# The second weight slab of the next job, split half a product ahead of its old place

## The chip, the cores and the metric

The kernel runs on one core of a Trainium2 chip. The metric is the device time of one execution in microseconds (us); lower is better. A program that is run again gives a slightly different time, so a median of runs is used, and one execution was also taken with the hardware profiler.

The engines are named as the profile names them: PE (the matrix engine), PEld (its weight loads), DVE (the vector engine), ACT (the scalar engine), POOL (GpSimd), SP (the engine whose queue issues most DMAs). Each engine takes its own instructions strictly in the order in which the program issued them to it, and waits only where an input is not there or a buffer is not free.

## The reference, cut to what matters

Two layers of a diffusion-style trunk over 512 latent tokens and, in the first layer, 256 context tokens of width 1024:

```python
for l in range(2):
    h, hc = trunk_layer(h, hc, ...)
def trunk_layer(x, ctx, ...):
    z_lat = split_proj(jnp.dot(layer_norm(x) * (1.0 + sc_l) + sh_l, w_in) + b_in)
    z_ctx = split_proj(jnp.dot(layer_norm(ctx) * (1.0 + sc_c) + sh_c, w_in) + b_in)
    ...
    y_f = fourier_mix(z_lat[0], fnet_w)
    y_d = diff_attn_latent(dq_l, ..., lam, diff_subln, lambda_init)
    y_p = pool_mix(z_lat[6], pool_w, pool_scale)
    y_n = na_latent(...)
    out_lat = gate_and_merge(z_lat, (y_f, y_d, y_p, y_n), w_branch, w_out)
    x_new = layer_norm(alpha * x + g_l * out_lat, ln_g, ln_b)
```

All is float32. Most of the work is products with the weights `w_in` (1024 x 10240), `w_branch` and `w_out`.

## The kernel before, in words

A float32 matrix is taken as the sum of a rounded "high" part and a "low" remainder, and a product as three matmuls: high by high, high by low, low by high. The normalised tokens lie on chip as such a pair (tiles `px0h`, `px0l` or `px1h`, `px1l`). The weights come in slabs of 512 rows by 256 columns (512 KB). A slab is fetched into one of three raw buffers (`w_raw`, DMA at line 319 in SP's queue). ACT then casts each of its two halves to the high part (`w_hi`, line 339), and DVE or POOL subtracts to get the low part (`w_lo`, line 342). There are four buffers for the split pair. Which engine subtracts is fixed per kind of job and half: both halves on POOL for the token sections (`tok`, `tok2`) and the plain sections (`nat`); the first half on POOL and the second on DVE for `rope` and `out`; both on DVE for gate sections, `merge`, `mgate`, `mproj`.

The program is a list of jobs, each a product of all tokens with some slabs:

- `tok2` and `tok`: token tiles of 128 rows are the outer loop; one "unit" is one tile by 256 columns, eight steps `k` of three matmuls
- `nat`, `rope`, `mgate`: two products `f` = 0, 1 of 128 weight columns each, eight steps `k` of three passes over all tokens (768 in layer 0, 512 in layer 1 for most)
- `merge`: two gate products and two branch products, three slabs; `mproj`: one slab
- `out`: units again. In layer 0 the token tiles fall in a first group of four tiles and a second of two; in layer 1 in two groups of two tiles. So a job has four units in the one case, and two in the three others; the last job of layer 1 has two column blocks, four units and four slabs

Most jobs use two slabs, here A (rows 0 to 511, needed from `k` = 0) and B (from `k` = 4). While a job runs, `ws.ahead(1)` splits A of the next job and `ws.ahead(2)` splits B. A split does this at its place in the program: it issues the raw DMA of the slab two further on (in a buffer that the slab just before the split one frees, and whose split is forced to its end first if it is not done), casts the first half on ACT, and starts a small chain: 0.6 planner-us later the subtraction of the first half and the cast of the second, 0.6 later the subtraction of the second. The planner's clock counts matmul time alone, 0.32 per step `k` of a unit.

All other work is placed by the same clock. After each step, chains that are due are issued (`pump`), and side work, that is the Fourier branch, differential attention and neighbourhood attention, is issued piece by piece between the steps of the section jobs. In the `out` jobs, evacuation of a unit is on DVE (multiply from the accumulator, line 1633; add the residual `xs`, line 1636; statistics, line 1639), and when a token tile has all its columns, a row chain `end_row` normalises it: small DVE steps, a power on POOL (line 578), a scaling on ACT (line 1656), a multiplication by `lng` (line 1659, on POOL for the four tiles of the first group), an addition on DVE (line 1662), and in layer 0 a second normalisation, transposes on PE (line 278), a scaling on ACT (line 606) and the split into the next layer's pair on DVE. The residual tiles `xs` have three buffers, and are fetched from SP's queue at the head of each unit.

Of the kernel before, what the change touches and what calls it, by code (L numbers as in the profile page):

```python
# [109 lines left out]
def emit(tc, A, out):  # L110
# [41 lines left out]
    def group(l, g):  # L152
        t = toks(l)
        return t[:-2] if g == 0 else t[-2:]
# [8 lines left out]
    for j in J:  # L163
# [7 lines left out]
        elif j[0] in ("merge", "mgate", "mproj"):  # L171
            _, l, b, s = j
# [9 lines left out]
    with ExitStack() as ctx, tc.manual_schedule():  # L182
# [30 lines left out]
        def finish(c, upto=None):  # L213
            while c.i < (len(c.st) if upto is None else upto):
                one(c)
# [50 lines left out]
        def mmt():  # L266
            return ring("mm", psA, [128, 512])
# [12 lines left out]
        def mm3(o, ah, al, bh, bl, start, stop):  # L280
            mm(o, ah, bh, start, False)
            mm(o, ah, bl, False, False)
            mm(o, al, bh, False, stop)
# [130 lines left out]
        ws = Stream(early)  # L414
# [204 lines left out]
        def gen_T(ps, hs, cols, X, chunks, nk, after=None, before=None):  # L619
            for k in range(nk):  # L620
                if before:
                    before(k)
                wh, wl = hs[k // 4]
                wh, wl = wh[:, k % 4, cols], wl[:, k % 4, cols]
                for j, (o, n) in enumerate(chunks):
                    mm(ps[j][:, :n], wh, X[0][:, k, o:o + n], k == 0, False)
                yield
                for j, (o, n) in enumerate(chunks):
                    mm(ps[j][:, :n], wh, X[1][:, k, o:o + n], False, False)
                yield  # L630
                for j, (o, n) in enumerate(chunks):
                    mm(ps[j][:, :n], wl, X[0][:, k, o:o + n], False, k == nk - 1)
                if after and k == after[0]:
                    after[1]()
                yield

        def chunks(n):
            return [(0, 512), (512, 256)] if n == T0 else [(0, 512)]
# [47 lines left out]
        def bias_row(l, c0):  # L686
            bb = sm.tile([128, 256], F32, name="bb", tag="bb")
            nc.sync.dma_start(bb, A["b_in"][l:l + 1, c0:c0 + 256].broadcast_to([128, 256]))
            return bb

        def job_tok(l, sec, s, X, F):
            hs = ws.take(2)
            bb = bias_row(l, sec * 512 + s * 256)
            tl = [4, 5, 0, 1, 2, 3] if (sec != 0 or l == 0) else [0, 1, 2, 3]
            for t in tl:
                if t == tl[0]:
                    mid = lambda: ws.ahead(1)
                else:
                    mid = (lambda: ws.ahead(2)) if t == tl[-1] else None
                yield from tok_unit(l, sec, s, t, X, F, hs, bb, mid)  # L700

        def job_tok2(l, sec, X, F):

            hs = ws.take(2)
            bb = [bias_row(l, sec * 512 + s * 256) for s in range(2)]
            for t in [4, 5, 0, 1, 2, 3]:
                if l == 0:
                    need(f"xt{t}")
                else:
                    finish_cls("out")  # L710
                    finish(rows_[t])
                finish(xt[t])
                for s in range(2):
                    if t == 4 and s:
                        hs += ws.take(2)
                    yield from tok_unit(l, sec, s, t, X, F, hs[2 * s:2 * s + 2], bb[s],
                                        (lambda: ws.ahead(2)) if (t == 3 and s == 1) else None)

        def evac_rope(l, sec, g, ps, ch, n, b, mt, cos, sin):

# [37 lines left out]
        def job_nat(l, sec, s, X, mt, tables=None):  # L758
            hs = ws.take(2)
            n = T0 if (sec in (3, 9) or l == 0) else NL  # L760
            ch = chunks(n)
            for f in range(2):
                ps = [mmt() for _ in ch]
                yield from gen_T(ps, hs, slice(f * 128, (f + 1) * 128), (X.h, X.l), ch, 8,
                                 after=((3, lambda: ws.ahead(1)) if f == 0 else (5, lambda: ws.ahead(2))))
                ct = sec * 4 + s * 2 + f
                b = biasT[l][:, ct:ct + 1]
                if sec in (2, 3):
                    evac_rope(l, sec, 2 * s + f, ps, ch, n, b, mt, *tables)
                elif sec in (8, 9):  # L770
                    evac_qk(l, sec, s, f, ps, ch, n, b, mt)
                elif sec == 6:
                    pool_group(l, 2 * s + f, ps, ch, n, b, mt)
                else:
                    evac_gate(l, sec, s, f, ps, ch, n, b, mt)
# [212 lines left out]
        def finish_cls(name):  # L988
            for c in klass.get(name, []):
                finish(c)  # L990
# [533 lines left out]
        def gate(l, b, dt_, ps, ch, sg):  # L1524
            ct = 48 + BR[b] * 8 + dt_

            def sig():
                for j, (o, m) in enumerate(ch):
                    S.activation(sg[:, o:o + m], ps[j][:, :m], AF.Sigmoid, bias=biasT[l][:, ct:ct + 1])  # L1529

            return chain((0.4, sig), hold=ps)
# [40 lines left out]
        def job_mgate(l, b, s, X, mp, sgs):  # L1572
            n = TQ[l]
            hs = ws.take(2)
            ch = chunks(n)
            for f in range(2):
                ps = [mmt() for _ in ch]
                yield from gen_T(ps, hs, slice(f * 128, (f + 1) * 128), X, ch, 8,
                                 after=((3, lambda: ws.ahead(1)) if f == 0 else (5, lambda: ws.ahead(2))))
                dt_ = 2 * s + f  # L1580
                sgs[dt_] = mp.tile([128, T0], F32, name="sgs", tag=("sg", "sg", "mtmp", "mtmp", "my", "my", "mg", "mg")[dt_], bufs=2)
                gate(l, b, dt_, ps, ch, sgs[dt_])
# [23 lines left out]
        def job_out(l, g, qs, M, ep, yt, gb, bst, lng, lnb):  # L1606
            hs_ = ws.take(2 * len(qs))
            units = [(t, q) for t in group(l, g) for q in qs]
            rows = list(gate_rows(l, gb, ep)) if (g, qs) == (0, (0,)) else []
            for i, (t, q) in enumerate(units):  # L1610
                cs = slice(q * 256, (q + 1) * 256)
                hs = hs_[2 * (q - qs[0]):][:2]
                ts = slice(t * 128, (t + 1) * 128)
                xs = ep.tile([128, 256], F32, name="xs", tag="xs", bufs=3)
                src = hres[ts, cs] if l else (A["x"][0, ts, cs] if t < 4 else A["ctx"][0, (t - 4) * 128:(t - 3) * 128, cs])
                nc.sync.dma_start(xs, src)
                ps = mmt()
                for k in range(8):
                    wh, wl = hs[k // 4]
                    mm3(ps[:, :256], M.h[:, k, ts], M.l[:, k, ts], wh[:, k % 4, :], wl[:, k % 4, :], k == 0, k == 7)  # L1620
                    if k == 3:
                        if i == 0 and len(qs) == 1:
                            ws.ahead(1)
                        if i == len(units) - 1:
                            ws.ahead(2)
                    if k % 2 == 0 and k // 2 < len(rows) and i < 2:
                        rows[k // 2][i]()
                    yield
                y = yt[t][:, cs]

                def gate_(y=y, ps=ps, t=t, cs=cs):
                    finish_cls("gate")
                    V.tensor_tensor(out=y, in0=ps[:, :256], in1=gb[0 if t < 4 else 1][:, cs], op=ALU.mult)  # L1633

                def add(y=y, xs=xs):
                    V.scalar_tensor_tensor(out=y, in0=xs, scalar=ALPHA, in1=y, op0=ALU.mult, op1=ALU.add)  # L1636

                def stats(y=y, t=t, q=q):
                    V.bn_stats(bst[t][:, q, :], y)
                    if q == 3:  # L1640
                        rows_[t] = end_row(l, t, yt[t], bst[t], lng, lnb, ep)

                chain(((3.6, 1.8)[i] if rows and i < 2 else 0.4, gate_), (0.41, add), (0.4, stats), hold=[ps], cls="out", depth=1)
# [105 lines left out]
        def need(flag):  # L1749
            while flag not in flags:  # L1750
                if not side_step(True):
                    assert pend, (flag, want)
                    finish(pend[0])
                    raise_flags()
# [28 lines left out]
        for j in J:  # L1783
# [81 lines left out]
            elif kind == "rope":  # L1865
                if not cs_:
                    need("fw")
                    late_tables()
                drive(job_nat(l, j[2], j[3], X, mt, cs_))
            elif kind == "nat":  # L1870
                drive(job_nat(l, j[2], j[3], X, mt))
# [65 lines left out]
```

## Time and profile before

| | us |
|---|---|
| runs | 2005.49, 2010.09, 2010.26 |
| their median | 2010.09 |
| the profiled execution, its own time | 2006.96 |
| its span, first to last instruction | 2005.2 |
| mean granted clock of PE, share of full speed | 0.976 |

The profile is one execution. Its page gives each engine's busy time; other views of the same trace list what each engine waited for ("waits"), the busy time in a stretch ("windows"), and the instructions in order of time ("timeline"). An idle stretch carries, after an arrow, the instruction that ended it. In the timeline a row may stand for several equal instructions in succession (x2, x3).

### The profile page before, as it was taken

Reading aid. Unit: us, or ns where it says so; the run is one execution under the profiler, and the core shown is the slowest. Engines: PE = TensorE matmul, PEld = TensorE weight load, DVE = VectorE, ACT = ScalarE, POOL = GpSimd, SP = SyncE. Lnnn points to the kernel's source line nnn. Section 1 sums busy time; section 2 is a strip of 40 time slices with the busy share of each in tenths; the row PEclk is TensorE's granted clock in tenths of the full one; section 3 lists DMA queues with packets and bytes.
Section 4 is the critical chain, followed back from the end, with each engine's and each line's share of the span. In section 5 each row is a group of like instructions: output and inputs, shape, how many; then the busy total and the mean of one; then the engine's idle time right before and its main releaser. Section 6 shows DMA issues by size and latency. Waiting matters only on the chain.

```text
span 2005.2 us, 30691 instructions
## 1 busy us (share of the span) xinstructions
PE 1901.0 (95%) x11703; PEld 1653.8 (82%) x11703; DVE 1185.4 (59%) x2369; ACT 861.7 (43%) x1673; POOL 329.9 (16%) x322
## 2 busy tenths in 40 slices
PE   6999999997999999999999979998999999999996
PEld 4998888776888888888888979877877887888886
DVE  7635676563666444656537784577655664465267
ACT  5423365564666422212223354355555664333232
POOL 6321121101120000000001443122122210000023
PEclk8999999998999999999999979999999999999999
DMA  8433844435453524434322446364327645444344
GB/s 275 132 103 108 250 135 152 161 108 163 154 160 106 181 96 136 137 107 152 99 95 96 132 150 193 103 237 137 124 100 236 210 135 183 136 159 137 94 132 152
DMA packets 257394, 293.71 MB, mean 146 GB/s; under 512 B 25844, under 2 KB 220384, under 8 KB 256736
## 3 DMA queue, kind: packets, MB, share of 16 engines
q1 hardware_dynamic: 256672, 286.46, 44.5%
q0 software_dynamic: 576, 5.29, 0.7%
q8 instruction: 92, 1.51, 0.3%
q14 instruction: 54, 0.44, 0.1%
HBM read 230.82 MB, written 62.35 MB: 146 GB/s over the span
## 4 chain that ended last, share of the span: by engine, by line
PE 52%; DVE 7%; DMA 2%; ACT 2%; issue 2%; POOL 1%; SPq 1%; POOLq 0%; ACTq 0%; DVEq 0%
PE mm L274 46%; PE sd L274 4%; PE sd L278 1%; DVE yt L1636 1%; DVE w_lo L342 1%; DMA w_raw<-in_w_out 1%; PE mm L394 1%; DVE px0l L286 1%; DVE dp L1013 1%; DMA mtmp<-y 1%; ACT px0l L1104 0%; DMA px0h<-nv1h 0%; DVE dp L1030 0%; DVE yt L1633 0%; DMA w_vec<-in_w_mod 0%
## 5 line engine op out<-in xcount | busy, mean ns | idle before, releaser
L342 POOL TENSOR_TENSOR w_lo<-w_raw,w_hi 128x512 fp32r<-128x512 f32 x148 | 209.3, 1425 | 1202.0 <-ACT w_hi L339 1129.6
L339 ACT CAST w_hi<-w_raw 128x512 fp32r<-128x512 f32 x456 | 263.6, 618 | 184.5 <-PE mm L274 120.3
L274 PE MATMUL mm<-px0h,w_hi 128*128 128x512 f32 x1216 | 336.4, 349 | 3.7 <-ACT px0h L1485 3.3
L274 PE MATMUL mm<-px0h,w_lo 128*128 128x512 f32 x1216 | 335.8, 349 | 0.0
L274 PE MATMUL mm<-px0l,w_hi 128*128 128x512 f32 x1216 | 334.1, 347 | 0.4 <-DVE px0l L1489 0.4
L342 DVE TENSOR_TENSOR w_lo<-w_raw,w_hi 128x512 fp32r<-128x512 f32 x308 | 220.1, 735 | 152.0 <-ACT w_hi L339 149.9
L274 PE MATMUL mm<-px1h,w_hi 128*128 128x512 f32 x864 | 291.8, 374 | 1.4 <-ACT sg L1529 1.4
L274 PE MATMUL mm<-px1h,w_lo 128*128 128x512 f32 x864 | 288.0, 369 | 0.0
L274 PE MATMUL mm<-px1l,w_hi 128*128 128x512 f32 x864 | 287.6, 369 | 0.0
L274 PEld LDWEIGHTS mm<-px0h,w_hi 128*128 128x128 f32 x1216 | 192.0, 190 | 34.5 <-ACT px0h L1485 4.5
L274 PEld LDWEIGHTS mm<-px0h,w_lo 128*128 128x128 f32 x1216 | 191.4, 190 | 32.2 <-issue 1.2
L274 PEld LDWEIGHTS mm<-px0l,w_hi 128*128 128x128 f32 x1216 | 192.4, 190 | 30.7 <-DVE px0l L1489 1.5
L274 PEld LDWEIGHTS mm<-px1h,w_hi 128*128 128x128 f32 x864 | 149.5, 189 | 30.6 <-ACT sg L1529 1.9
L274 PEld LDWEIGHTS mm<-px1h,w_lo 128*128 128x128 f32 x864 | 149.5, 189 | 28.3 <-issue 1.3
L274 PEld LDWEIGHTS mm<-px1l,w_hi 128*128 128x128 f32 x864 | 149.6, 189 | 26.8 <-issue 0.5
L274 PE MATMUL mm<-w_hi,px0h 128*128 128x256 f32 x480 | 143.1, 298 | 4.3 <-DVE px0h L610 4.0
L274 PE MATMUL mm<-w_lo,px0h 128*128 128x256 f32 x480 | 139.3, 290 | 6.7 <-POOL w_lo L342 6.0
L274 PE MATMUL mm<-w_hi,px0l 128*128 128x256 f32 x480 | 138.9, 289 | 0.7 <-DVE px0l L286 0.7
L274 PE MATMUL mm<-w_lo,px1h 128*128 128x256 f32 x384 | 112.5, 293 | 8.4 <-DVE w_lo L342 4.7
L274 PE MATMUL mm<-w_hi,px1h 128*128 128x256 f32 x384 | 114.2, 297 | 2.1 <-ACT w_hi L339 1.7
L274 PE MATMUL mm<-w_hi,px1l 128*128 128x256 f32 x384 | 111.5, 290 | 0.2 <-DVE px1l L286 0.2
L1529 ACT ACTIVATE sg<-mm,biasT 128x512 f32<-128x512 f32 x72 | 41.8, 615 | 153.8 <-PE mm L274 123.3
(240 smaller groups left out, 3100.2 us busy)
## 6 DMA issues: line engine op xcount, KB each, us to landing
w_raw<-in_w_in SPq DMA_DIRECT2D x160, 512.0 KB, 4.2
w_vec<-in_w_mod SPq DMA_DIRECT2D x32, 512.0 KB, 3.6
w_raw<-in_w_branch SPq DMA_DIRECT2D x32, 512.0 KB, 3.5
w_raw<-in_w_out SPq DMA_DIRECT2D x32, 512.0 KB, 3.5
w<-in_w_mod SPq DMA_DIRECT2D x12, 512.0 KB, 6.2
g<-ab SPq DMA_DIRECT2D x16, 384.0 KB, 2.7
nb<-bt SPq DMA_DIRECT2D x48, 128.0 KB, 4.5
y<-y SPq DMA_DIRECT2D x14, 384.0 KB, 3.7
```

What stands on the lines that cost most here:

```text
L274: PE.matmul(o, a, b, start=start, stop=stop)
L278: PE.transpose(o, i, idn)
L286: V.tensor_tensor(out=out_lo, in0=src, in1=hi.bitcast(F32), op=ALU.subtract)
L339: S.copy(x[1], x[0])
L342: e.tensor_tensor(out=x[2], in0=x[0], in1=x[1].bitcast(F32), op=ALU.subtract)
L394: PE.matmul(st["p"][:, 4 * b + 2 * v:4 * b + 2 * v + 2], acc[:, v, b * 128:(b + 1) * 128], ones[:, 0:2].bitcast(F32), start=True, stop=True)
L1013: V.tensor_scalar(out=p, in0=src, scalar1=-0.125, scalar2=None, op0=ALU.mult, op1=ALU.min, accum_out=mn)
L1529: S.activation(sg[:, o:o + m], ps[j][:, :m], AF.Sigmoid, bias=biasT[l][:, ct:ct + 1])
L1636: V.scalar_tensor_tensor(out=y, in0=xs, scalar=ALPHA, in1=y, op0=ALU.mult, op1=ALU.add)
```

## The change

`ws.ahead(2)`, the split of slab B of the next job, is issued earlier in five places. Everything else, and the place of `ws.ahead(1)`, stays:

```diff
 (job_tok)
-                    mid = (lambda: ws.ahead(2)) if t == tl[-1] else None
+                    mid = (lambda: ws.ahead(2)) if t == tl[-3] else None
 (job_tok2)
-                                        (lambda: ws.ahead(2)) if (t == 3 and s == 1) else None)
+                                        (lambda: ws.ahead(2)) if (t == 2 and s == 1) else None)
 (job_nat, and the same line in job_mgate)
-                                 after=((3, lambda: ws.ahead(1)) if f == 0 else (5, lambda: ws.ahead(2))))
+                                 after=((3, lambda: ws.ahead(1)) if f == 0 else (1, lambda: ws.ahead(2))))
 (job_out)
-                        if i == len(units) - 1:
+                        if i == max(len(units) - 3, 0):
                             ws.ahead(2)
```

In a `tok` job the place is two units earlier, in `tok2` one tile (two units), in `nat`, `rope` and `mgate` four steps `k` earlier within the second product. In an `out` job of four units it is two units earlier; in one of two units it goes from the second unit to the first, right behind `ws.ahead(1)` of the same step. The split of B forces the chain of A to its end there, since B's raw DMA wants A's buffer. `merge` and `mproj` jobs are not touched.

## Rows read from the trace of the kernel before

**Rows 1.** The page of the profile: busy time, share of the span and instructions of each engine.

```profile
PE 1901.0 (95%) x11703; PEld 1653.8 (82%) x11703; DVE 1185.4 (59%) x2369; ACT 861.7 (43%) x1673; POOL 329.9 (16%) x322
```

**Rows 2.** The waits of PE over the whole run: who waited for what, us in total, times, longest.

```profile
PE mm L274 <- POOL w_lo L342: 15.1, 9, 3.7
PE sd L274 <- DVE px0l L286: 12.2, 11, 3.5
PE sd L274 <- DVE px1l L286: 9.5, 10, 3.0
PE sd L278 <- DVE np L1329: 8.5, 4, 4.0
PE mm L274 <- DVE w_lo L342: 6.6, 6, 3.2
PE mm L274 <- ACT w_hi L339: 5.2, 4, 2.6
```

**Rows 3.** The same view by stretches, columns as before: first three rows from 0 to 52 us, the next three from 1139 to 1183, one from 1183 to 1226, the last two from 1935 to the end.

```profile
PE mm L274 <- POOL w_lo L342: 5.6, 4, 2.4
PE mm L274 <- ACT w_hi L339: 3.5, 3, 2.6
PE mm L274 <- DVE w_lo L342: 1.2, 2, 0.6
...
PE mm L274 <- POOL w_lo L342: 6.0, 2, 3.7
PE sd L278 <- ACT yt L1656: 3.7, 1, 3.7
PE mm L274 <- DVE w_lo L342: 0.7, 1, 0.7
...
PE mm L274 <- POOL w_lo L342: 2.8, 2, 1.8
...
PE mm L274 <- DVE w_lo L342: 4.7, 3, 3.2
PE mm L274 <- ACT w_hi L339: 1.7, 1, 1.7
```

**Rows 4.** Windows: start and end, length, busy us (and instructions) of PE, PEld, DVE, ACT, POOL, then the granted PE clock, the DMA engines' share and GB/s.

```profile
1144.60:1189.60 45.00, 31.86 (x202) 30.43 (x201) 39.86 (x75) 27.72 (x56) 26.54 (x19) 0.79 0.41 130
...
1968.10:1989.70 21.60, 14.46 (x99) 13.43 (x98) 15.65 (x29) 5.78 (x10) 10.07 (x7) 0.92 0.47 152
```

**Rows 5.** The timeline of ACT: start us, us, engine, line, operation, tiles, shapes, count, and the idle time before it. The first row is the last step of `tok2` in layer 0, the others the four-unit `out` jobs of layer 0.

```profile
89.32 1.14 ACT L339 CAST w_hi<-w_raw 128x512 fp32r<-128x512 f32 x2 [0.58 <-PE mm L274]
...
1114.59 1.14 ACT L339 CAST w_hi<-w_raw 128x512 fp32r<-128x512 f32 x2 [8.94 <-PE mm L274]
...
1126.11 1.14 ACT L339 CAST w_hi<-w_raw 128x512 fp32r<-128x512 f32 x2 [8.94 <-PE mm L274]
```

**Rows 6.** The timeline of POOL in the two-unit `out` jobs of layer 0, and one row of PE's. Same columns.

```profile
1141.72 1.47 POOL L342 TENSOR_TENSOR w_lo<-w_raw,w_hi 128x512 fp32r<-128x512 f32 x1
...
1144.12 3.00 POOL L1659 TENSOR_TENSOR yt<-yt,lng 128x1024 f32<-128x1024 f32 x1
1147.08 1.44 POOL L342 TENSOR_TENSOR w_lo<-w_raw,w_hi 128x512 fp32r<-128x512 f32 x1
...
1148.58 0.39 PE L274 MATMUL mm<-w_lo,px0h 128*128 128x256 f32 x1 [2.27 <-POOL w_lo L342]
...
1150.58 3.01 POOL L1659 TENSOR_TENSOR yt<-yt,lng 128x1024 f32<-128x1024 f32 x1
1153.56 1.48 POOL L342 TENSOR_TENSOR w_lo<-w_raw,w_hi 128x512 fp32r<-128x512 f32 x1
```

**Rows 7.** The timeline of the last `out` jobs of layer 1, rows of ACT, DVE and SP (whose rows are the issue of a DMA). Same columns.

```profile
1965.16 1.13 ACT L339 CAST w_hi<-w_raw 128x512 fp32r<-128x512 f32 x2
...
1971.40 1.64 ACT L339 CAST w_hi<-w_raw 128x512 fp32r<-128x512 f32 x3
...
1974.20 1.41 DVE L342 TENSOR_TENSOR w_lo<-w_raw,w_hi 128x512 fp32r<-128x512 f32 x1
...
1976.58 1.05 DVE L1636 SCALAR_TENSOR_TENSOR yt<-xs,yt 128x256 f32<-128x256 f32 x1
1977.67 0.43 DVE L1639 BATCH_NORM_STATS2 st<-yt 128x6 f32<-128x256 f32 x1
1978.01 0.67 DVE L342 TENSOR_TENSOR w_lo<-w_raw,w_hi 128x512 fp32r<-128x512 f32 x1
...
1978.75 0.38 SPq L319 DMA_DIRECT2D w_raw<-in_w_out  x1
...
1984.96 1.66 ACT L339 CAST w_hi<-w_raw 128x512 fp32r<-128x512 f32 x3 [3.70 <-DMA w_raw<-in_w_out]
```

**Rows 8.** The timeline of DVE in the four-unit `out` jobs of layer 0 (first and second row) and at the head of the two-unit ones (third). Same columns.

```profile
1102.05 0.42 DVE L1636 SCALAR_TENSOR_TENSOR yt<-xs,yt 128x256 f32<-128x256 f32 x1
...
1105.73 1.33 DVE L342 TENSOR_TENSOR w_lo<-w_raw,w_hi 128x512 fp32r<-128x512 f32 x1
...
1139.49 2.55 DVE L1636 SCALAR_TENSOR_TENSOR yt<-xs,yt 128x256 f32<-128x256 f32 x1
```

**Rows 9.** The timeline of ACT in a section job of layer 0 with differential attention beside it: the copy of a transposed tile, and behind it the casts of a slab B. Same columns.

```profile
431.97 0.80 ACT L1104 CAST px1l<-sd 128x768 fp32r<-128x768 f32 x1 [0.71 <-PE sd L278]
432.67 1.14 ACT L339 CAST w_hi<-w_raw 128x512 fp32r<-128x512 f32 x2
```

More of the change, by code (lines that the diff above doesn't have):

```diff
@@ L1578, in job_mgate @@
                 yield from gen_T(ps, hs, slice(f * 128, (f + 1) * 128), X, ch, 8,
-                                 after=((3, lambda: ws.ahead(1)) if f == 0 else (5, lambda: ws.ahead(2))))
+                                 after=((3, lambda: ws.ahead(1)) if f == 0 else (1, lambda: ws.ahead(2))))
                 dt_ = 2 * s + f
```

## The prediction, made before the changed kernel was run

> **What bounds the kernel now.** I read the page first: PE is busy 1901.0 of 2005.2 us, so all its idle time together is 104 us [rows 1]. A change that issues the same work in another order can only take from that, or from stretches where PE ran at its lower clock. Next I read what PE waited for. Weights are the smaller part: 15.1 us for low parts from POOL, 6.6 from DVE and 5.2 for high parts from ACT, 26.9 together. Inputs of the side work's products make 12.2, 9.5 and 8.5 [rows 2]. Then the same view by stretches, to see where the weight waits lie: 5.6 + 3.5 + 1.2 = 10.3 us in the first 52 us, where `mod` jobs run that the change leaves alone; 6.7 from 1139 to 1183 and 2.8 from 1183 to 1226; and from 1935 on 4.7, 1.7 and what is left, 26.9 - 10.3 - 6.7 - 2.8 - 6.4 = 0.7 [rows 3]. So from 52 to 1139 and from 1226 to 1935, where most of the moved splits are, PE never waits for a weight: slab B is in time there already. The change can gain directly only at the two `out` phases and at the head of layer 1.
>
> Those places are not PE's alone. From 1144.6 to 1189.6 DVE is busy 39.86 of 45.0 us and PE 31.86, at a mean granted clock of 0.79. From 1968.1 to 1989.7 DVE has 15.65 and PE 14.46 of 21.6 [rows 4].
>
> **The change part by part.** No instruction is added or removed; each moved split takes along one raw DMA in SP's queue, two casts on ACT and two subtractions.
>
> *Four-unit `out` jobs, `tok2`.* Nothing. ACT runs ahead of PE here, and its casts begin when PE has read the old slab in the buffer for the last time: 8.94 us idle until PE, at 1114.59 and again 11.52 us later [rows 5]. That is one job of four units, so a unit takes 2.88 us, and a half slab, two of its eight steps, 0.72. An earlier place in the program changes no such release. In `tok2` the cast at 89.32 already waits for PE's last use [rows 5]; after the change the same wait stands ahead of two evacuation casts in ACT's order, and DVE and SP wait behind these for some 6 us. Four accumulators, 4 x 2.88 = 11.5 us of units, hide that; without them it would cost up to 2.9, one unit, in each layer.
>
> *Two-unit `out` jobs of layer 0.* POOL's order is: first half of A (1141.72), a row's multiplication (1144.12, 3.00 us), first half of B (1147.08). PE stands 2.27 us for the last, then 0.7 for DVE's half [rows 3, 6]. Planner times put B's half behind A's and ahead of that multiplication after the change: ready at 1141.72 + 1.47 + 1.44 = 1144.6, wanted at 1148.58 - 2.27 = 1146.3. Both waits go, 2.97 us. The following job's longest wait, 6.0 - 2.27 = 3.7, is for its B behind a second multiplication [rows 3], and goes in the same way. What is late next is that job's A: it stays behind the multiplication of 1150.58 and is ready at 1153.56 + 1.48 = 1155.0 [rows 6], and PE, without waits, would want it after two units from 1144.6, at 1150.4. So up to 4.6 of 6.7 us comes back. The wait of 3.7 for `yt` (transposes behind the row chain) I take to shorten by 1, bounds 0 and 3.7; of the 2.8 at the head of layer 1, where `tok2`'s B comes late, I take 1.5, bounds 0 and 2.8 [rows 3]. Sum: 6.7 - 4.6 + 1 + 1.5 = 4.6. Its upper bound is 45.0 - 39.86 = 5.1 while DVE's busy time stays [rows 4]; its lower one 6.7 - 4.6 = 2.1, or nothing if A's wait also slows the clock. I take 4.5.
>
> *Last `out` jobs of layer 1.* B's first half is cast with A's second (1965.16, x2), its second only at 1971.40, behind a row's scaling, and DVE subtracts that at 1974.20 to 1975.6; PE waits 4.7 in all for DVE [rows 3, 7]. Moved up, its cast comes behind A's, and its subtraction goes in DVE's order ahead of an addition, an evacuation and a row's two long steps, which I put at 1970.1. It is wanted 6 steps of 0.36 after 1968.1, at 1970.3: about 4 us of waiting go. But the last slab's DMA is issued (1978.75) when DVE has subtracted from the slab whose buffer it takes (1978.01), lands 6.2 us later, and PE waits for that too [rows 3, 7]. DVE has no idle time up to there, so the release moves only past one residual addition and one statistics step, 1.05 + 0.43 = 1.5 us earlier. Less crowded, its DMA could land sooner: up to 4 in all. I take 2.5 between 1.5 and 4.
>
> *Sections and `mgate`.* Forecast: nothing. Cover is PE's own matmuls: a B split late costs no wait today, and one split earlier has more slack. On ACT the pair of casts (1.14 us) moves from one place among the attention's copies to another [rows 9]. In tok 10, nat 9 and 8, and the gate sections, 14 jobs a layer, 28 pairs run beside attention. A pair may leave the path of a copy that PE waits for or step into one: bounds ±28 x 1.14 = ±32 us; the direct waits that it can lengthen or shorten are 30.2 [rows 2]. With no reason for a sign I take 0, ±3.
>
> *SP's queue.* In a two-unit job, the second unit's `xs` now comes behind B's DMA, which waits for A's last subtraction. DVE is late itself there, so I put nothing; without that cover at most 1 us in each of 10 jobs (four in layer 0, six in layer 1).
>
> Sum: 4.5 + 2.5 = 7.0. From the profiled execution's 2006.96 that gives 2000.0. The median shown is 3.1 above that execution; I set the forecast halfway, **2001.5 us**, with a range of its own of 1996 to 2005.
>
> **The rivals.** *One: DVE stays the bound.* DVE's work isn't less, and now A's DVE half runs while POOL works on B's first half. A subtraction took 1.33 us in such company and 0.67 without [rows 7, 8], so six two-unit jobs (four of layer 0, the last two of layer 1) give back 6 x 0.66 = 4.0 of the 7.0: 2004 on the execution's scale, 2005.5 on mine. For it: the residual addition of 0.42 took 2.55 while POOL multiplied, and DVE is full there [rows 4, 8]. Against it: half of these meetings exist today. The Trainium skill says the same, as a rule, in "SBUF — State Buffer", section "Who interferes with whom": a DVE instruction with two SBUF inputs and a GpSimd one that reads SBUF shut each other out whole. By that rule back-to-back halves cost as much as this rival says, and the 2.55 us agrees with it.
>
> *Two: slower.* B's casts land ahead of attention copies on ACT, for which PE then stands. It has to happen, net, to more than 7.0 / 1.14 = 6 of the 28 pairs to eat the gain; with 13 it costs 14.8 - 7.0 = 7.8, 2015 on the execution's scale, 2016 on mine. For it: PE already waits 30.2 us for such inputs, so that chain has no slack [rows 2]. Against it: pairs stand among those copies today as well, such as the one right behind a copy at 432.67 [rows 9], and moving them frees as many places as it fills.
>
> *Three: all goes.* The waits of 6.7, 3.7, 2.8 and 7.1 vanish, 20.3 us, nothing coming back: 1988. Against it: the late A worked out above, and the last DMA.
>
> *That the move does nothing* in the places that count, since engines run at the release of buffers, is the four-unit case; with two units the order on POOL and DVE decides, so I leave it within the first rival.
>
> **How the numbers follow.** Forecast 0.45, rival one 0.27 (2004 to 2010, taking in no effect), two 0.20 (2010 to 2024), three 0.08 (1985 to 1995). A measurement of this kernel tells about 0.3%, 6 us, from no change, so faster means below 2004.1 and slower above 2016.1. Faster: 0.8 of the forecast's chance, all of three, little of one: 0.36 + 0.08 + 0.01 = 0.45. Slower: 0.8 of rival two and a little of mishap beside: 0.17. Same: 0.38. The range 1992 to 2012 leaves out about 0.05 below and 0.13 above.
>
> **What would show it.** In the changed kernel's profile the POOL wait of 2.27 at the first unit of layer 0's second two-unit job must be gone, with the multiplication now behind two subtractions; a wait for A of the next job should appear near 1151. In layer 1 the wait near 1975 for DVE's low part should shrink to under 1 us, and the last slab's DMA be issued 1 to 2 us sooner relative to the end. If PE's weight waits after 1139 still add up to over 12 us, rival one holds or the order isn't what I worked out; if waits for px or np parts exceed 38 us in all, rival two.

## The result, and the profile of the changed kernel

| | us |
|---|---|
| the changed kernel, median of 6 runs | 2025.80 (2019.60 to 2029.74) |
| the kernel before, median of 6 runs | 2009.71 (2005.49 to 2011.26) |
| ratio of the two | 1.0078, 95% interval 1.0061 to 1.0096 |
| profiled execution, its own time; span; mean granted clock | 2021.72; 2019.9; 0.978 |

The change made the kernel slower by 0.78 per cent, some 16 us. The forecast was 2001.5 us, a gain, with a range that ended at 2012.

Busy time by engine of the changed kernel, the first part of its page, answering to [rows 1]:

```profile
PE 1902.0 (94%) x11703; PEld 1656.2 (82%) x11703; DVE 1190.6 (59%) x2369; ACT 860.4 (43%) x1673; POOL 330.4 (16%) x322
```

PE's own work is the same within 1 us, and DVE takes 5.2 us longer over its instructions. What grew is waiting. The waits of PE over the whole run (who for whom, us in total, times, longest), answering to [rows 2]:

```profile
PE mm L274 <- POOL w_lo L342: 15.4, 9, 4.5
PE sd L274 <- DVE px1l L286: 11.5, 9, 3.0
PE sd L274 <- DVE px0l L286: 11.5, 11, 3.1
PE sd L278 <- DVE np L1329: 7.2, 4, 3.8
PE sd L278 <- ACT yt L1656: 7.0, 3, 3.7
PE mm L274 <- ACT w_hi L339: 7.0, 4, 3.3
PE mm L274 <- DVE vt L654: 5.6, 2, 3.4
...
PE mm L274 <- DVE w_lo L342: 4.6, 5, 1.5
```

Three things are to be seen. The inputs of attention, 11.5 + 11.5 + 7.2 = 30.2 us, are what they were. Waits for weights, 15.4 + 7.0 + 4.6 = 27.0, are too (26.9 before): the change removed some and made others. New are `vt`, 5.6 us, which is PE waiting for an accumulator that DVE has not evacuated, and `yt`, the scaled row that PE transposes, 7.0 instead of 3.7.

Where the time went, worked out from the end of the last matmul of each stage in the two traces:

| stage | difference, us |
|---|---|
| `mod` | -2.4 |
| `tok2` and the first `tok` jobs, layer 0 | +4.4 |
| rest of layer 0 up to the `out` jobs | +0.9 |
| `out` of layer 0, `tok2` of layer 1 | +5.9 |
| first `tok` jobs, layer 1 | +5.1 |
| rest of layer 1 up to the `out` jobs | -1.1 |
| `out` of layer 1 | +1.9 |

They add up to the 14.7 by which the spans differ. The first line is no effect of the change: the traces of all kernels below show it too, -0.9 to -2.5. One trace against one other is not exact in the long section stages: in kernels whose edit leaves the sections alone a layer's sections differ from the kernel before by -1.8 to +7.2.

**The head of each layer.** The chain is told by a few rows of three timelines (start us, us, engine, line, operation, tiles, count, idle time before; SPq and the DMA rows are the issue of a transfer). First the changed kernel:

```profile
82.03 8.99 SPq L319 DMA_DIRECT2D w_raw<-in_w_in  x2
87.38 1.14 ACT L339 CAST w_hi<-w_raw 128x512 fp32r<-128x512 f32 x2 [6.34 <-PE mm L274]
...
93.36 0.52 SPq L832 DMA_DIRECT2D pw<-in_pool_w  x1
93.43 0.75 POOL L898 DMA_DIRECT2D px1h<-in_k_tabh  x1
93.97 0.56 SPq L688 DMA_DIRECT2D bb<-in_b_in  x1
94.18 0.53 POOL L899 DMA_DIRECT2D px1l<-in_k_tabl  x1
...
104.82 0.42 DVE L654 TENSOR_TENSOR vt<-mm,bb 128x256 f32<-128x256 f32 x1 [7.18 <-DMA bb<-in_b_in]
105.30 0.39 PE L274 MATMUL mm<-w_hi,px0h 128*128 128x256 f32 x1 [2.18 <-DVE vt L654]
...
1249.18 0.36 PE L274 MATMUL mm<-w_hi,px1h 128*128 128x256 f32 x1 [3.39 <-DVE vt L654]
```

Then the kernel before, whose PE was some 2 us later at this point:

```profile
90.10 2.86 SPq L319 DMA_DIRECT2D w_raw<-in_w_in  x2
93.05 0.46 SPq L832 DMA_DIRECT2D pw<-in_pool_w  x1
93.60 0.45 SPq L688 DMA_DIRECT2D bb<-in_b_in  x1
...
95.19 0.75 POOL L898 DMA_DIRECT2D px1h<-in_k_tabh  x1
95.94 0.54 POOL L899 DMA_DIRECT2D px1l<-in_k_tabl  x1
...
98.82 0.42 DVE L654 TENSOR_TENSOR vt<-mm,bb 128x256 f32<-128x256 f32 x1 [3.23 <-DMA bb<-in_b_in]
```

In `tok2` the moved split issues its raw DMA early. The buffer of that DMA comes free only when POOL has subtracted slab A, POOL waits for ACT's casts of A, and these wait until PE has done with the old slab (ACT idle for 6.34 us, until 87.38). So SP, which takes its queue in order, is held for 9 us. Behind it stand four stores, the pool weights `pw`, and `bb`, the bias row of the next job. Before, `bb` (128 KB) was issued 1.6 us ahead of the two Fourier tables (1292 KB each, from POOL's queue), and DVE had it 5.2 us later (98.82 - 93.60). Now it is issued 0.5 us behind the first table, and DVE has it after 10.9 us. DVE cannot evacuate without it; four accumulators last for 11.5 us of units, and PE stands for 2.18 us, then runs 3.4 us at half its clock (granted 0.50, 1.2 of 2.4 GHz). In layer 1 the same chain costs 3.4 us of waiting (the row at 1249.18).

**The two-unit `out` jobs.** PE's waits from 1139 to 1235, answering to rows 4 to 7 of [rows 3]:

```profile
PE mm L274 <- POOL w_lo L342: 8.4, 3, 4.5
PE sd L278 <- ACT yt L1656: 7.0, 3, 3.7
PE mm L274 <- ACT w_hi L339: 1.9, 1, 1.9
```

Before, these were 6.7 + 2.8 for weights and 3.7 for `yt`, 13.2 together; now they are 17.3. The waits of 2.27 and 0.7 for B are gone, and that job ends 4.8 us earlier against its predecessor. The next job gives it all back, and more: PE waits for its A, 1.92 for the high part and 3.37 for the low one. Rows of ACT and PE:

```profile
1155.19 1.24 ACT L1656 ACTIVATE yt<-yt,nm,rs 128x1024 f32<-128x1024 f32 x1 [5.29 <-DVE nm L589]
1156.33 2.16 ACT L339 CAST w_hi<-w_raw 128x512 fp32r<-128x512 f32 x4
1156.99 0.39 PE L274 MATMUL mm<-w_hi,px0h 128*128 128x256 f32 x1 [1.92 <-ACT w_hi L339]
...
1160.74 0.58 PE L274 MATMUL mm<-w_lo,px0h 128*128 128x256 f32 x1 [3.37 <-POOL w_lo L342]
...
1986.87 0.82 ACT L1656 ACTIVATE yt<-yt,nm,rs 128x512 f32<-128x512 f32 x1 [5.76 <-DVE nm L589]
1987.59 2.17 ACT L339 CAST w_hi<-w_raw 128x512 fp32r<-128x512 f32 x4
```

All four casts, A's and B's, stand behind a row scaling for which ACT waited 5.29 us, and that scaling waits for the row's mean from DVE. In layer 1 (the last two rows) it is much the same picture: the job before the last gains 5.0 us and the last one loses 6.0, with four of its casts behind a scaling at 1986.87 that had waited 5.76 us for DVE, and a stretch of 6.83 us at half clock (the granted clock from 1997.41 to 2004.24 is 0.50).

### The profile page after: what moved, and what is told of

Same layout as the page of the kernel before. It is cut to its first block, busy times and chain, and to the rows that moved or that the text cites. A ratio compares the mean times of both kernels' runs of the same rounds, so it can differ in the third digit from the quotient of the medians.

```text
span 2019.9 us, 30717 instructions
## 1 busy us (share of the span) xinstructions
PE 1902.0 (94%) x11703; PEld 1656.2 (82%) x11703; DVE 1190.6 (59%) x2369; ACT 860.4 (43%) x1673; POOL 330.4 (16%) x322
## 3 DMA queue, kind: packets, MB, share of 16 engines
q0 software_dynamic: 576, 5.29, 0.7%
## 5 line engine op out<-in xcount | busy, mean ns | idle before, releaser
L274 PE MATMUL mm<-w_lo,px1h 128*128 128x256 f32 x384 | 113.0, 294 | 10.7 <-POOL w_lo L342 7.2
L274 PEld LDWEIGHTS mm<-w_hi,px0h 128*128 128x128 f32 x480 | 97.2, 202 | 12.8 <-DVE px0h L610 4.5
```

What stands on the lines that cost most here:

```text
L274: PE.matmul(o, a, b, start=start, stop=stop)
```

## The experiments

All ratios are against the kernel before, run beside them; one per cent is 20.1 us.

**Which of the moves costs?** Three kernels, each with a part of the change alone:

```diff
 (tok2_only)
-                                        (lambda: ws.ahead(2)) if (t == 3 and s == 1) else None)
+                                        (lambda: ws.ahead(2)) if (t == 2 and s == 1) else None)
 (out_only)
-                        if i == len(units) - 1:
+                        if i == max(len(units) - 3, 0):
 (sections_only)
-                    mid = (lambda: ws.ahead(2)) if t == tl[-1] else None
+                    mid = (lambda: ws.ahead(2)) if t == tl[-3] else None
-                                 after=((3, lambda: ws.ahead(1)) if f == 0 else (5, lambda: ws.ahead(2))))
+                                 after=((3, lambda: ws.ahead(1)) if f == 0 else (1, lambda: ws.ahead(2))))
```

> Only the place in tok2 is moved. Theory Q (SP's queue): the raw DMA of the moved split holds SP for some 9 us, the bias row bb of the next job is issued behind it and behind two table transfers, and PE stands in the first tok job of each layer for an accumulator: gaps of 2.2 and 3.4 us there plus the half clock after each, as in the changed kernel, so slower by 7 to 10 us. Rival A (attention copies): the cost of the change lies in the section jobs; then this kernel is within 3 us of before.

> Only the place in the out jobs is moved. Theory D (DVE's and ACT's order): the gain at the first two-unit job comes back at the next, where the next A is cast behind a row scaling that waits for DVE; the two out phases together cost 5 to 9 us. The forecast of record said -7. Rival A: within 3 us of before or faster.

> Only the places in tok, nat, rope and mgate are moved, 28 pairs of casts beside attention among them. Theories Q and D: no net cost, within 3 us of before. Rival A: slower by 10 us or more, with waits of PE for attention inputs over 38 us.

| | ratio | interval | us |
|---|---|---|---|
| `tok2_only` | 1.0053 | 1.0035 to 1.0070 | +10.7 |
| `out_only` | 1.0030 | 1.0016 to 1.0044 | +6.0 |
| `sections_only` | 1.0013 | 1.0001 to 1.0024 | +2.6 |

The parts add up to 19, within their intervals of the whole's 16. More than half of the loss comes from one changed line, the one in `tok2`, and its trace shows the same waits as the whole change (2.4 for `vt` in each layer). The sections, where 28 pairs of casts moved, cost at most little, and their waits for attention inputs did not grow (11.5 + 11.5 + 6.2 = 29.2).

**Why does `tok2` cost?** Two kernels leave the moved split where it is, and take away one later link each: the first issues the next job's bias row ahead of the split, the second issues the Fourier tables 4 planner-us later.

```diff
 (tok2_bias_first)
+            def early_bb_and_split():
+                early_bb.append(bias_row(l, 0))
+                ws.ahead(2)
 (tok2_tables_last)
-            G.dma_start(F.fh[:, 0:2584], A["k_tabh"])
-            G.dma_start(F.fl[:, 0:2584], A["k_tabl"])
...
-                yield 19.2
+                yield 4.0
+                G.dma_start(F.fh[:, 0:2584], A["k_tabh"])
+                G.dma_start(F.fl[:, 0:2584], A["k_tabl"])
+                yield 15.2
```

> As tok2_only, with the bias row of the next job issued ahead of the moved split (a third bb buffer). Theory Q: DVE's wait for bb goes, PE's gaps of 2.2 and 3.4 us in the first tok jobs go, and the time is within 3 us of before. Rival C (the casts that stand ahead of two evacuation casts in ACT's order, or SP's stall of the spills): the gaps stay, and so does the cost of 7 to 10 us.

`tok2_bias_first` came to 1.0032 (1.0018 to 1.0046), +6.4 us, less than `tok2_only` but not free. Both waits for `vt` are gone; in layer 0 nothing replaced them, and there the stage cost nothing. In layer 1 it still cost 4.7 us. The row of ACT that tells why:

```profile
1240.74 0.62 ACT L842 CAST pwh<-pw 128x512 fp32r<-128x512 f32 x1 [5.63 <-DMA pw<-in_pool_w]
```

The pool weights were issued behind the tables too, and ACT stood at their cast with evacuations and weight casts queued behind it. So the theory was widened: it is not the bias row but everything that SP issues behind the held DMA and so behind the tables.

> As tok2_only, with the two table transfers of the Fourier branch issued 4 planner-us later, so behind pw and bb of the next job. Theory Q, widened by tok2_bias_first (there ACT waited 5.6 us for pw, with evacuations and casts of weights behind it): what costs is that SP, held for 8 to 9 us, issues bb and pw behind the tables; then both gaps go and the time is within 3 us of before. Rival C: SP's stall itself, or the casts ahead of evacuations, costs; then slower by 5 us or more as tok2_bias_first.

`tok2_tables_last` came to 0.9998 (0.9988 to 1.0008): nothing is left of the cost. Its rows:

```profile
82.33 9.00 SPq L319 DMA_DIRECT2D w_raw<-in_w_in  x2
...
94.31 0.59 SPq L688 DMA_DIRECT2D bb<-in_b_in  x1
...
98.49 0.43 DVE L654 TENSOR_TENSOR vt<-mm,bb 128x256 f32<-128x256 f32 x1 [0.63 <-DMA bb<-in_b_in]
98.97 0.75 POOL L904 DMA_DIRECT2D px1h<-in_k_tabh  x1
```

SP is held for the same 9 us and the bias row is issued as late as in the changed kernel, but DVE has it 4.2 us after its issue. SP's stall, and the casts ahead of the evacuations, cost nothing by themselves. What cost was the order of transfers behind them. The later tables alone, without the moved split, were not run; but in this trace `tok2` and the first `tok` jobs take 0.4 us longer than before in layer 0 and 0.1 in layer 1, so no gain by the tables hides a cost there.

**Why do the `out` jobs cost?** The first theory was that DVE is full there. Windows over the same stretch of work, from DVE's first evacuation in the two-unit jobs of layer 0 to its last (start and end, length, busy us and instructions of PE, PEld, DVE, ACT, POOL, granted clock, DMA share, GB/s); the kernel before, in the whole stretch and in its first part:

```profile
1139.03:1186.34 47.31, 36.02 (x243) 34.79 (x241) 43.49 (x76) 28.96 (x59) 29.02 (x19) 0.82 0.43 137
...
1139.03:1170.76 31.73, 25.07 (x174) 24.25 (x173) 31.08 (x53) 14.95 (x26) 23.07 (x15) 0.84 0.42 137
```

and `out_only`:

```profile
1141.38:1192.01 50.63, 36.85 (x249) 35.84 (x247) 45.07 (x77) 29.42 (x59) 30.24 (x19) 0.83 0.37 119
```

DVE was busy 31.08 of the first 31.73 us before the change. After it the stretch is 3.3 us longer, of which DVE is busy for 1.6 and idle for 1.7. So kernels were made in which POOL's subtractions go to DVE (`low_dve`), POOL's multiplications go to DVE (`mul_dve`), or the rows of layer 0 leave out their multiplication and addition (`light`, which so computes something else), each with the old place and with the moved one:

```diff
 (low_dve)
-SHARED = {"rope": 1, "tok2": 2, "out": 1, "tok": 2, "nat": 2, "gate": 0, "mod0": 1}
+SHARED = {"rope": 1, "tok2": 2, "out": 0, "tok": 2, "nat": 2, "gate": 0, "mod0": 1}
 (mul_dve)
-E_POOL = ((4, 5, 0, 1), ())
+E_POOL = ((), ())
 (light, layer 0)
-(0.32, lambda: norm("a")), (2.4, mul), (2.4, add), (2.0, again),
+(0.32, lambda: norm("a")), (6.8, again),
```

> The kernel before, with both low halves of the out slabs on DVE, none on POOL. Theory D (DVE is full in the two-unit out jobs of layer 0, 31.08 of 31.73 us, and sets their pace): PE's waits for POOL there turn into waits for DVE, and the time is 0 to 6 us longer. Rival P (POOL's order, subtractions behind the row multiplications, sets the pace): PE's 6.0 us of waiting for POOL go with nothing in their place, 3 to 8 us faster.

> The kernel before, with the row multiplications of the first group on DVE instead of POOL. DVE takes on 4 x 1.21 us in layer 0, and five residual additions that took 2.1 to 2.6 us beside a multiplication fall to 0.42. Theory D with contention: DVE's sum falls by some 5 us there, and the time by 3 to 8 us. If contention is not what stretches the additions, DVE's sum grows by 4.8 us and the time by 3 to 6 us.

> Both: the out jobs' place moved as in out_only, and the row multiplications on DVE. Theory D: with DVE's load lowered the moved split costs nothing or gains, so within 3 us of mul_dve. Rival S (the place itself is bad, since the next A is cast behind a row scaling): 4 to 8 us slower than mul_dve, as out_only is against before.

> The out jobs' place moved, and both low halves of the out slabs on DVE, so that POOL never subtracts beside DVE there. Theory T (contention: A's and B's subtractions now come as a pair, and POOL's pair stretches DVE's steps, 0.68 to 2.1 us, just where a row's statistics are due): against low_dve the move then costs at most 2 us. Rival S (the order on ACT: the next A's casts stand behind a row scaling that waits for DVE, whoever subtracts): it costs 4 to 7 us against low_dve, as out_only does against before.

> A diagnostic that leaves out part of the computation: the multiplication by lng and the addition of lnb in the rows of layer 0 (the rows of layer 1 keep theirs). DVE loses 1.21 us per row and the stretched additions of 2.1 to 2.6 us, POOL 3.0 us per row. Theory R (the row work on DVE sets the pace of layer 0's two-unit out jobs): the waits there shrink and the time falls by 6 to 12 us against before. If PE's weights set the pace, only those behind a multiplication on POOL go, 3 to 6 us.

> The out jobs' place moved, with the same part left out as in light. Theory R: with DVE's row work lighter the move no longer costs in layer 0; what is left is layer 1's share (1.7 us in the profile of out_only), so within 4 us of light. Rival O (the move costs by its order alone, whatever DVE has to do): 5 to 8 us slower than light, as out_only is against before.

| base | place as before | place moved | the move costs |
|---|---|---|---|
| the kernel before | 1 | 1.0030 | 0.30% |
| `mul_dve` | 0.9997 (0.9986 to 1.0008) | 1.0027 (1.0013 to 1.0041) | 0.30% |
| `low_dve` | 0.9974 (0.9961 to 0.9986) | 1.0009 (0.9997 to 1.0021) | 0.35% |
| `light` | 0.9952 (0.9934 to 0.9970) | 0.9989 (0.9978 to 1.0001) | 0.37% |

The last column is the quotient of the two before it, uncertain by some 0.2. None of this helped: the move costs 6 to 7 us whoever subtracts, whoever multiplies, and also when a row needs neither multiplication nor addition. Expectations missed on the way: `mul_dve` gained nothing, since DVE's own multiplications ate what the unstretched additions gave (it is busy for 1185.4 us in both), and `low_dve`, which gives DVE more to do, is the fastest full kernel of the study. That DVE's load alone sets the pace fell with it; `light` shows that the rows do weigh, 9.6 us in all.

What the move does is best seen in `light` and `out_light`, for in `light` weights are late by only 1.1 us in the two-unit jobs of layer 0. Waits of PE over the whole run, `light` and then `out_light`:

```profile
PE mm L274 <- POOL w_lo L342: 9.6, 7, 2.5
...
PE mm L274 <- DVE w_lo L342: 6.8, 6, 3.6
PE sd L278 <- ACT yt L1656: 3.4, 1, 3.4
PE mm L274 <- ACT w_hi L339: 3.0, 2, 2.8
```

```profile
PE mm L274 <- POOL w_lo L342: 13.5, 11, 4.6
...
PE sd L278 <- ACT yt L1656: 7.7, 4, 3.1
...
PE mm L274 <- ACT w_hi L339: 5.2, 3, 2.6
PE mm L274 <- DVE w_lo L342: 3.0, 4, 1.3
```

With next to nothing to gain in layer 0, the moved split still makes its rows late: transposes wait 4.3 us more for scaled rows. PE's waits for weights over the whole run change less, from 19.4 to 21.7: 3.9 more for POOL's low parts and 2.2 for ACT's high parts, 3.8 less for DVE's low parts.

Three more theories were put to the test: that the next A, queued on ACT behind a row scaling, has to be cast earlier; that the split of B does harm because its raw DMA forces A's chain to its end on the spot; and that the weight work in `out` stands too early in any case.

```diff
 (a_early, out_a_early; a_late with k == 6)
+                    if k == 0 and i == 0 and len(qs) == 1:
+                        ws.ahead(1)
                     if k == 3:
-                        if i == 0 and len(qs) == 1:
-                            ws.ahead(1)
 (out_no_force)
-                        if i == len(units) - 1:
-                            ws.ahead(2)
+                        if i == max(len(units) - 3, 0):
+                            ws.split(ws.cur + 1, load=False)
+                        if i == len(units) - 1:
+                            ws.load(ws.cur + 3)
```

> The out jobs' place moved, and the split of A issued at step 0 of the first unit instead of step 3, so that A's first cast stands ahead of the second of two row scalings on ACT. Rival S: PE's wait for A's high part (1.9 us in out_only) goes, and the move costs 0 to 3 us against before. Theory T: the pair of subtractions is the same, and the time is within 3 us of out_only, 4 to 8 us slower than before.

> The kernel before with the split of A alone issued at step 0 of the first unit; B stays. No theory has a strong claim here: A is not late in the kernel before (PE waits for B there), so S and T both say within 3 us of before. It shows what of out_a_early is due to A alone.

> As out_only (B's casts and subtractions at the moved place), but the raw DMA that the split of B issues, and with it the forced end of A's chain, stays at the old place. Theory F: in the moved kernels that forced end puts A's last subtraction on DVE ahead of a unit's residual addition and row statistics, where it waits for ACT's casts (DVE idle 1 to 1.5 us at each in the profile of out_light), and everything of the row comes later; without it the cost against before falls from 6.4 us to under 2.5, or to a gain. Rival P (the place of B's casts and subtractions itself): still 5 to 8 us slower than before.

> The same with both low halves on DVE, against low_dve (0.26 per cent faster than before; moved with the forced end, 0.09 per cent slower than before). Theory F: within 3 us of low_dve, so faster than before by 2 us or more. Rival P: 5 to 8 us slower than low_dve, that is as slow as before or slower.

> The kernel before, with the split of A issued at step 6 of the first unit instead of step 3 in the out jobs. If weight work stands too early there (a_early cost 0.22 per cent), 1 to 5 us faster than before; if the present place is the best one, A's low part comes late and it is 1 to 5 us slower.

| | ratio | interval |
|---|---|---|
| `a_early` | 1.0022 | 1.0010 to 1.0034 |
| `out_a_early` | 1.0036 | 1.0024 to 1.0048 |
| `out_no_force` | 1.0032 | 1.0021 to 1.0042 |
| `low_dve_out_no_force` | 1.0025 | 1.0012 to 1.0038 |
| `a_late` | 1.0015 | 1.0002 to 1.0029 |

All three fell. A cast earlier costs 4 us by itself, and the moved B on top of it still some 3 (0.14 per cent, within its uncertainty nothing or all of the rest); without the forced end the cost is as large as with it, also on the base of `low_dve` (0.51 per cent there). And A later costs 3 us, only just clear of nothing. So by these runs the cost goes with the place of B's casts and subtractions among the row work; its DMA, one engine's load and POOL's company don't explain it, and an earlier A doesn't mend it. Of the way in which it costs only an account from the order of instructions is left, argued and not shown. ACT's order in the two-unit jobs of layer 0, the kernel before against the changed one, as their traces run (other instructions left out):

```
 L1656 ACTIVATE yt, first row
-L339 CAST w_hi x2
 L1656 ACTIVATE yt, second row
-L339 CAST w_hi x2
+L339 CAST w_hi x4
 L1656 ACTIVATE yt, third row
-L339 CAST w_hi x2
 L1656 ACTIVATE yt, fourth row
-L339 CAST w_hi x2
+L339 CAST w_hi x4
```

Before, each unit brings one row to scale and one slab to cast in turn, so each wait for DVE holds up one slab. After, two rows are scaled, and then both slabs of the next job come at once. PE gets nothing until the second row is through, then has weights for two units, and the rows of those two fall to DVE together. One run speaks against this as the whole account: in `out_a_early` ACT scales one row at a time, with one and three casts between, and still its transposes wait 9.8 us for scaled rows (3.8 in `a_early`, whose casts are grouped alike), and its two-unit jobs with the `tok2` behind them take 4.9 us longer than before (4.2 in `out_only`). A kernel that casts B early and keeps two casts to each row was not tried. Why the `out` jobs cost stays open.

**A version that beats both.** `low_dve` alone, 0.9974, is 5 us faster than the kernel before. Its profile does not say where: PE's waits for weights there are 28.1 us, not fewer, and the `out` jobs of both layers with the `tok2` between them take what they took, within 0.1 us; the 3.9 us by which its last matmul ends earlier lie in `mod` and the sections, which the edit leaves alone. So why it is faster stays open. Two attempts to better it:

> low_dve with A early, as a candidate: low_dve was 0.26 per cent faster than before. If A's place is free, as both theories say, this is within 3 us of low_dve, so 3 to 8 us faster than before.

> low_dve with A at step 6, the other candidate: by the same reasoning 1 to 5 us faster or slower than low_dve, which was 0.26 per cent faster than before.

They came to 0.9996 (0.9985 to 1.0007) and 0.9981 (0.9970 to 0.9992), not better than `low_dve`.

## Why the prediction was wrong

Two terms of the sum failed. `tok2`, put at nothing because the accumulators would cover the stall, costs 10.7 us when it is moved alone. The `out` jobs, put at a gain of 4.5 + 2.5, cost 6.0 when they are moved alone. Of the first the runs show the cause, of the second only the place.

**Sections and `mgate`: right within its bounds.** Nothing ± 3 us was forecast, +2.6 was measured alone (interval 0.2 to 4.8). That rival two's mechanism, casts ahead of attention copies, would be the way to a loss was wrong: the sum of waits by which it was to be recognised stayed at 30.2, far from 38. Its sign came true by other places.

**Four-unit `out` jobs: right.** After the first, each takes the same time in both traces within 0.1 us.

**`tok2`: the first step that failed.** The prediction saw the wait and where it would stand: ahead of two evacuation casts, with SP held behind it, and "four accumulators, 4 x 2.88 = 11.5 us of units, hide that". The cover was counted against the length of the stall alone, 6 us estimated and 9 measured. What was queued on SP behind it was not followed to its landing: the bias row, issued 2.3 us later against PE, met 2.6 MB of tables and took 5.6 us longer. The price of a lost cover was put at up to 2.9 in each layer; the waits were 2.2 and 3.4, and with the clock and what followed the stages cost 4.4 and 5.1. `tok2_tables_last` shows this term whole: 10.7 us with the tables ahead, none with the tables behind.

**Two-unit `out` jobs of layer 0: the second.** The first steps held. POOL's multiplication stands behind two subtractions (1145.53, two in 3.18 us, then the multiplication at 1149.63), the waits of 2.27 and 0.7 are gone, and the predicted new wait for A came, 5.3 us where 4.6 were worked out. Then "The wait of 3.7 for `yt` (transposes behind the row chain) I take to shorten by 1" and "of the 2.8 at the head of layer 1, where `tok2`'s B comes late, I take 1.5" failed in sign: they grew to 7.0 and 5.1. Added up, the waits of this stage rose from 13.2 to 17.3 us, nearly all of the 4.2 that it lost. The upper bound, DVE's spare time of 45.0 - 39.86 = 5.1 us, was taken over a window whose end is not full; from 1139.03 to 1170.76 DVE had 0.65 us to spare. That DVE is full does not explain the loss, though: the move costs as much where DVE has less to do (`light`) and where it has more (`low_dve`). Why the rows came later instead of earlier stays open. Forecast -4.5, measured +5.9 in the two traces; 1.6 of that is the first four-unit job, partly at a lower clock (granted 0.50 from 1096.29 to 1099.70), and in `out_only`, without it, the stage lost 4.2.

**SP's queue in `out`: right.** SP is held for 11.78 us at 1149.32, and in the two-unit jobs of layer 0 no wait of DVE for `xs` appears.

**Last `out` jobs of layer 1: right up to the last job.** "About 4 us of waiting go": the job before the last gained 5.0. But the wait near 1975 became 1.5 us (at 1985.8), not under 1: B's second half is cast behind a row's scaling (at 1980.50) and subtracted at 1985.09, behind the row's two long steps on DVE and not ahead of them as forecast. And the last raw DMA was not issued 1 to 2 us sooner relative to the end: it was issued at 1993.03, 26.9 us before the end of the span, where it had been 26.5. The last job lost 6.0, by waits for A's and B's low parts behind the second row's scaling and by 6.83 us at half clock. Forecast -2.5, measured +1.9.

**Rival one** named DVE as the bound, and its row of stretched additions is real. The prediction's sign for it or for a wrong order, waits for weights of over 12 us after 1139, came true: they are 17.6 (16.6 before). But its price, 4.0 of the gain given back, was too small, and `out_mul_dve` and `out_low_dve`, each of which takes away one half of POOL's company, show that this company is not what makes the move cost. Its sentence on the Trainium skill ("SBUF — State Buffer", "Who interferes with whom") agrees with rows such as the subtraction of 2.08 us at 1157.49 in the changed kernel, beside POOL's multiplication from 1156.67 to 1159.02. The two kernels above show that this rule did not decide the case.

## What to carry to other kernels

When a step is moved ahead of others in a DMA queue, follow each transfer queued behind it to its landing, and look at what other queues issue at that moment: half a microsecond decided here which side of 2.6 MB a bias row came down. Before a wait of PE is counted as gain, work out the following jobs too, rows and weights both: the 4.8 us gained in one `out` job were paid back, with 4.2 more, in those behind it. Take a spare time over a window that ends where the full stretch ends. And where work alternates with a row chain in an in-order queue, read the order out after the move: here one row and two casts in turn became two rows and four casts, which may be what costs and is not shown.

## What the runs showed of the hardware that was not expected

How soon a small transfer can be used went, in these runs, with what another queue issued around it. The bias row of 128 KB, from SP's queue, reached DVE 5.2 us after its issue when the two tables followed it by 1.6 us, 4.2 us when they followed by 4.7, and 10.9 us when the first table went 0.5 us ahead from another queue. And a kernel with more work on the fuller engine was faster: `low_dve` has DVE busy for 1191.3 us instead of 1185.4 and POOL for 284.4 instead of 329.9, and gains 0.26 per cent, for a reason that its trace does not show.
